# A hybrid attention and state-space block in f32: the state-space branch's output product by one level of Strassen's scheme

## The chip, the cores and the metric

One Trainium2 chip; the kernel runs on one of its cores. The metric is the device time of one execution in microseconds (us), the median over several runs. The engines are TensorE (PE in the profile), VectorE (DVE), ScalarE (ACT), GpSimd (POOL) and SyncE (SP, which here only issues DMAs).

## The reference

One layer of a token mixer with three branches (latent attention "mla", forgetting attention "fox", a state-space scan "ssm"), each with its own output matrix and sigmoid gate, followed by a gated feed-forward part. Sequence length and model width are 1024; the two attention branches are 512 wide, the state-space branch 1024. What matters here:

```python
y_a = mla_branch(...) @ w_br_mla[l]        # [1024, 512]  @ [512, 1024]
y_b = fox_branch(...) @ w_br_fox[l]        # [1024, 512]  @ [512, 1024]
y_c = ssm_branch(...) @ w_br_ssm[l]        # [1024, 1024] @ [1024, 1024]
g = jax.nn.sigmoid(u_gate + b_gate[l]).reshape(Bsz, S, N_BRANCH, D_MODEL)
merged = g[:, :, 0] * y_a + g[:, :, 1] * y_b + g[:, :, 2] * y_c
x = x + merged @ w_out[l]
```

`ssm_branch` ends in an RMS norm with a gain per column (`norm_g`); everything is float32.

## The kernel before, in words

**Precision.** A float32 operand is used as two rounded tiles, a high part and a low part (`split`, L139: ACT copies the high part, DVE subtracts it for the low part). A product of two such operands is three matmul passes, high x high, high x low and low x high (`mm3`, L161, one matmul on L167). Each matmul here is 128 x 128 weights on 128 x 512 data.

**Before the stage.** The attention results wait in DRAM (`att_d`), and so do the gates (`g_d`) and the rows of the state-space branch (`ys_d`, stored transposed by L1219 in eight blocks of 128 tokens, the last of them just before the stage). Projections that were left over (`fill`, matmuls on L840, evacuated on L847) fill PE up to the first matmul of the stage.

**The stage that is changed** (L1244 to L1290) makes the merged rows, transposed: eight tiles `merged[j]` (`mg`) of 128 columns by 1024 tokens. It runs over the branches in the order fox, mla, ssm. For each branch the input rows are loaded (`ar`, L1257) and split into `ah` and `al` (L1260; for ssm with the norm's gain `pc_n` as a scale, L1261 and L1262). Then for each of the eight column tiles j the weights are loaded and split (`load_w`, L734: `wr`, `wh`, `wl`), the gate row is loaded (`gl`, L1272), and two halves of 512 tokens are computed: 12 matmuls each for fox and mla (4 blocks of 128 inputs x 3 passes), 24 for ssm. That is 192 + 192 + 384 = 768 matmuls, `ybr` in the profile. DVE evacuates each half, `(gate + 1) * psum` (L1279); for mla POOL adds it to `merged` (L1282), for ssm DVE does (L1284). In the ssm branch each finished row is at once rounded into `mh` and `ml` (the tiles `hnh` and `hnl`, L1285 and L1286), the operand of the output projection `wo`, which follows (weights `raw` loaded at L1394, split into `woh` and `wol`, matmuls on L1417).

**What sets the order.** In this stage a scheduler orders each engine's instructions; each engine then runs its own list strictly in order, and SP's list is the order in which DMAs are issued. A tile pool with n buffers makes the n+1-th tile wait for the readers of the first. `wr`, `wh` and `wl` have two buffers each, the pool with the tag `t4` (rows, gates) has four.

**Elsewhere in the kernel.** The feed-forward up projection already uses the seven-product scheme: its helper `product` runs the 12 matmuls of one block product, and `sums` (L1464 to L1470) lets POOL form the four sums of weight blocks.

## Time and profile before

| | |
|---|---|
| median of 3 runs | 2073.37 us (2071.99 to 2074.21) |
| profiled execution | 2070.99 us, its span 2069.3 us |
| granted TensorE clock, mean | 0.994 |
| busy share of the span | PE 97%, DVE 69%, ACT 46%, POOL 30% |
| moved by DMA | 303.62 MB, 147 GB/s on average |
| branch outputs of fox, mla and ssm | about 1151 to 1326 us, 8% of the chain |
| output projection and second norm | from 1326 us |

The span is what the profiler saw from the first to the last instruction; the execution's own time is 1.7 us longer. "The chain that ended last" follows the last instruction back to what released it, step by step. Each group row names the line, engine, operation and tiles, then how many instructions, busy time and mean duration, and at the end the idle time ahead of them and what ended it.

### The profile page before, as it was taken

Reading aid. Unit: us, or ns where it says so; the run is one execution under the profiler, and the core shown is the slowest. Engines: PE = TensorE matmul, PEld = TensorE weight load, DVE = VectorE, ACT = ScalarE, POOL = GpSimd, SP = SyncE. Lnnn points to the kernel's source line nnn. Section 1 sums busy time; section 2 is a strip of 40 time slices with the busy share of each in tenths; the row PEclk is TensorE's granted clock in tenths of the full one; section 3 lists DMA queues with packets and bytes.
Section 4 is the critical chain, followed back from the end, with each engine's and each line's share of the span. In section 5 each row is a group of like instructions: output and inputs, shape, how many; then the busy total and the mean of one; then the engine's idle time right before and its main releaser. Section 6 shows DMA issues by size and latency. Waiting matters only on the chain.

```text
span 2069.3 us, 29096 instructions
## 1 busy us (share of the span) xinstructions
PE 2014.6 (97%) x10265; PEld 1684.3 (81%) x10265; DVE 1425.6 (69%) x2595; ACT 950.5 (46%) x1739; POOL 616.9 (30%) x606
## 2 busy tenths in 40 slices
PE   6999899999999999999999999999899999999999
PEld 6989788788888888887778888888778888878887
DVE  5678579366667766757896355557987777775665
ACT  4555323156556666555554222323454444454432
POOL 2435233222222222210000040002654454422755
PEclk9999999999999999999999999999999999999999
DMA  5057878654344455324442665431222322329665
GB/s 175 18 175 252 261 225 248 199 158 142 105 126 110 134 133 133 101 82 135 134 134 82 217 207 167 154 121 63 84 89 81 95 79 72 102 88 338 231 227 195
DMA packets 276650, 303.62 MB, mean 147 GB/s; under 512 B 19308, under 2 KB 209784, under 8 KB 276504
## 3 DMA queue, kind: packets, MB, share of 16 engines
q1 hardware_dynamic: 276504, 301.76, 47.0%
q8 instruction: 81, 1.33, 0.3%
q14 instruction: 65, 0.53, 0.1%
HBM read 209.03 MB, written 92.67 MB: 146 GB/s over the span
## 4 chain that ended last, share of the span: by engine, by line
PE 84%; DVE 7%; DMA 5%; ACT 2%; issue 2%; SPq 0%; POOL 0%; DVEq 0%; ACTq 0%; POOLq 0%
PE mm L840 17%; PE dn L1703 10%; PE ybr L167 8%; PE ua L1371 5%; PE fx L167 5%; PE ud L1371 5%; PE uc L1371 5%; PE wo L1417 4%; PE s L930 4%; PE tp L999 3%; PE ub L1371 2%; PE fxv L167 1%; PE cq L167 1%; PE o L970 1%; PE kv L167 1%
## 5 line engine op out<-in xcount | busy, mean ns | idle before, releaser
L840 PE MATMUL mm<-hnh,wh 128*128 128x512 f32 x576 | 250.4, 435 | 0.0
L840 PE MATMUL mm<-hnh,wl 128*128 128x512 f32 x576 | 226.5, 393 | 0.0
L840 PE MATMUL mm<-hnl,wh 128*128 128x512 f32 x576 | 225.2, 391 | 0.0
L952 POOL TENSOR_SCALAR pm<-pm,rs 128x128 f32<-128x128 f32 (+7 forms) x128 | 107.9, 845 | 348.6 <-DVE rs L951 317.8
L1703 PE MATMUL dn<-dr,dr 128*128 128x512 f32 x592 | 182.2, 389 | 0.0
L1005 DVE TENSOR_TENSOR ptl<-tp,pth 128x512 fp32r<-128x512 f32 (+1 forms) x160 | 101.3, 633 | 83.8 <-ACT pth L1004 82.8
L935 DVE TENSOR_REDUCE nmx<-s 128x1 f32<-128x128 f32 (+2 forms) x192 | 105.7, 551 | 57.2 <-PE s L933 45.7
L945 ACT ACTIVATE pm<-s,nmx 128x128 f32<-128x128 f32 (+2 forms) x192 | 109.6, 575 | 55.9 <-DVE nmx L942 38.5
L1703 PEld LDWEIGHTS dn<-dr,dr 128*128 128x128 f32 x592 | 111.3, 188 | 23.0
L840 PEld LDWEIGHTS mm<-hnh,wl 128*128 128x128 f32 x576 | 108.0, 188 | 24.8
L840 PEld LDWEIGHTS mm<-hnl,wh 128*128 128x128 f32 x576 | 109.0, 189 | 18.4 <-issue 4.1
L840 PEld LDWEIGHTS mm<-hnh,wh 128*128 128x128 f32 x576 | 108.9, 189 | 17.8 <-issue 4.1
L1004 ACT ACTIVATE pth<-tp 128x512 fp32r<-128x512 f32 (+1 forms) x160 | 88.1, 551 | 69.4 <-PE tp L999 68.7
L930 PE MATMUL s<-qk,qk 96*128 96x384 f32 (+5 forms) x480 | 117.8, 350 | 0.9 <-ACT pm L945 0.9
L1282 POOL TENSOR_TENSOR mg<-mg,gl 128x512 f32<-128x512 f32 x16 | 24.9, 1558 | 306.5 <-DVE gl L1279 306.4
L1703 PE MATMUL dn<-dr 128*128 128x512 f32 x296 | 115.5, 390 | 0.0
L143 DVE TENSOR_TENSOR dr<-dr,dr 128x1024 fp32r<-128x1024 f32 x52 | 74.2, 1427 | 52.1 <-ACT dr L142 46.5
L167 PE MATMUL fx<-w5h,hnh 128*128 128x512 f32 x256 | 102.4, 400 | 1.7 <-ACT w5h L142 1.7
L167 PE MATMUL fx<-w5l,hnh 128*128 128x512 f32 x256 | 100.8, 394 | 2.0 <-DVE w5l L143 2.0
L167 PE MATMUL fx<-w5h,hnl 128*128 128x512 f32 x256 | 100.6, 393 | 0.0
L167 PE MATMUL ybr<-al,wh 128*128 128x512 f32 x256 | 99.2, 389 | 0.5 <-DVE al L143 0.5
L167 PE MATMUL ybr<-ah,wl 128*128 128x512 f32 x256 | 98.3, 389 | 0.0
(492 smaller groups left out, 5817.3 us busy)
## 6 DMA issues: line engine op xcount, KB each, us to landing
dr<-act_d SPq DMA_DIRECT2D x99, 256.0 KB
wr<-in_ffn_w_up_dram SPq DMA_DIRECT2D x47, 512.0 KB
wr<-in_w_in_dram SPq DMA_DIRECT2D x36, 512.0 KB
g_d<-t SPq DMA_DIRECT2D x24, 512.0 KB
gl<-g_d SPq DMA_DIRECT2D x24, 512.0 KB
ws<-in_ffn_w_down_dram SPq DMA_DIRECT2D x22, 512.0 KB
wsum_d<-ws SPq DMA_DIRECT2D x22, 512.0 KB
act_d<-fa SPq DMA_DIRECT2D x22, 512.0 KB
```

Source lines behind the costliest of these rows:

```text
L143: return i, le.tensor_sub(l, src, f32(h))
L167: T.matmul(ps, a(k), b(k), start=(i == 0), stop=(i == n - 1))
L840: T.matmul(ps, a[:, k, :], b[half][:, k, :], start=(k == 0 and i == 0), stop=(k == NK - 1 and i == 2))
L930: T.matmul(ps[:, :w], q_[:, qs], k_[:, a:a + w], start=i_ == 0, stop=not last and i_ == len(o.passes) - 1)
L935: later(c + 0.1, lambda ps=ps, ci=ci, a=a, b=b: V.reduce_max(nmx[:, ci:ci + 1], ps[:, :b - a], axis=AX, negate=True))
L945: pss[ci][1][0] = later(c + 0.9 + 0.1 * ci, lambda ci=ci, a=a, b=b: A.activation(p_[:, a:b], pss[ci][0][:, :b - a], AF.Exp, bias=nb, accum ...
L952: G.tensor_scalar(p_[:, 0:n * P], p_[:, 0:n * P], rs[:, 3:4], 0.0, op0=ALU.mult, op1=ALU.add)
L1004: later(c + 0.05, lambda th=th, pt=pt, off=off: A.activation(th[:, :off], pt[:, :off], AF.Copy))
L1005: pl[0] = later(c + 0.6, lambda th=th, tl=tl, pt=pt, off=off: V.tensor_sub(tl[:, :off], pt[:, :off], f32(th[:, :off])))
L1371: T.matmul(ps, a, b, start=first and n == 0, stop=n == 11, skip_group_check=not first)
L1417: T.matmul(p, a, b, start=k == 0 and i == 0, stop=k == NK - 1 and i == 2)
L1703: T.matmul(ps[m], a[:, ts_], b[:, 512:], start=first_ and j == 0 and q == 0, stop=j == NFH - 1 and q == 2, skip_group_check=not first_)
```

## The change

For pairs of column tiles (j, j + 4) and the two token halves, the ssm branch's four 128 x 512 outputs are made from seven block products instead of eight (Winograd's form of Strassen's scheme). A block product has 512 inputs: 12 matmuls. Four pairs x 7 x 12 = 336 matmuls take the place of 384. The scheme needs four sums of input blocks (`tsum`, made once) and four sums of weight blocks per pair (`S12`, `S34`), and its products are combined on the way out.

- **Token sums.** `tok_sums(n)`, called eight times (before fox column tiles 1 to 7 and before mla column tile 0), loads 128-column pieces of four blocks from `ys_d` into the one tile `tr` (pool with one buffer, two DMAs of 256 KB), scales them by the norm's gain on ACT, forms two differences on POOL and two on DVE, and splits the four results. The parts go into `mh` and `ml`, which stand empty until the merged rows are rounded.
- **Plain blocks.** `tok_block`, called six times (four in mla, two behind it), loads and splits the three unsummed blocks. The eight loads of full ssm rows are gone.
- **Pairs.** Each pair loads both weight tiles and both gate rows; POOL makes `S12` (in the buffer of `tr`) and `S34` (in a `t4` buffer). PE's order within the pairs is written by hand. Combining takes ACT copies out of PSUM, DVE and POOL adds, and the same gate multiply and merge add as before.
- **Rounding.** The merged rows stay in f32 until the last pair (`tail`), since `mh` and `ml` hold the token sums; all 16 roundings now stand in that pair.
- Helpers `product`, `rows` and `weight_sums` move up, and the feed-forward part uses them from there.

The core of the diff:

```diff
+        def tok_sums(n):
+            k, q = n // 2, n % 2 * 256
+            r = trp.tile([P, 4, 256], F32, name=uid("tr"), tag="tr")
+            for i in range(2):
+                SY.dma_start(r[:, 2 * i:2 * i + 2, :],
+                             ys_d[k + 4 * i].rearrange("p (h c) -> p h c", h=2)[:, :, q:q + 256])
+                A.activation(r[:, 2 * i:2 * i + 2, :], r[:, 2 * i:2 * i + 2, :], AF.Copy,
+                             scale=pc_n[:, k + 4 * i:k + 4 * i + 1])
+            a1, a2, b1, b2 = (r[:, i, :] for i in range(4))
+            G.tensor_sub(a1, a2, a1)
+            G.tensor_sub(a2, b2, a2)
+            V.tensor_sub(b2, b2, a1)
+            V.tensor_sub(b1, b1, b2)
+            for i, t in ((2, b2), (1, a1), (3, a2), (4, b1)):
+                h, l = (x_[k][:, q:q + 256] for x_ in tsum[i])
+                split(h, l, t)
...
             for j in range(NK):
-                wh, wl = load_w(fpl, wv[:, :, j * P:j * P + P], nk)
+                if b == 1 and j or b == 0 and j == 0:
+                    tok_sums(j - 1 if b else 7)
+                if b == 0 and 1 <= j < 5:
+                    k = 2 * (j - 1)
+                    blocks += tok_block(k, 0, k // 4)
+                wh, wl = load_w(fpl, wv[:, :, j * P:j * P + P], 4)
...
-                    if b == 2:
-                        V.tensor_add(m, m, g[:, hs])
-                        i0 = A.activation(mh[half][:, j, :], m, AF.Copy, scale=0.5)
-                        i1 = V.scalar_tensor_tensor(out=ml[half][:, j, :], in0=m, scalar=0.5,
-                                                    in1=f32(mh[half][:, j, :]), op0=ALU.mult, op1=ALU.subtract)
...
+                hA = operand(ri)
+                S12 = trp.tile([P, NK, P], F32, name=uid("S12"), tag="tr")
+                S34 = fpl.tile([P, NK, P], F32, name=uid("S34"), tag="t4", bufs=4)
+                weight_sums(S12, S34, ri, rj)
+                a0 = halfbank()
+                product(a0, hA, 0, *Y11)
+                A.activation(e1, a0, AF.Copy)
+                hS12 = operand(S12)
+                b0 = halfbank()
+                product(b0, hS12, 4, *tsum[2])
+                V.tensor_add(X, b0, e1)
+                if tail:
+                    rounded(range(3), 0)
+                product(a0, hA, 4, *Y21, first=False)
+                add(a0, j, 0)
+                if tail:
+                    rounded((3,), 0)
+                hS34 = operand(S34)
+                h22 = last22[:, 0:4, :], last22[:, 4:8, :]
+                split(*h22, rj[:, 4:8, :])
+                c0_ = halfbank()
+                product(c0_, hS12, 0, *tsum[1])
+                A.activation(e5, c0_, AF.Copy)
+                if tail:
+                    rounded((4, 5, 6), 0)
+                d0 = halfbank()
+                product(d0, hS34, 0, *tsum[3])
+                A.activation(e7, d0, AF.Copy)
+                G.tensor_add(Y, e5, e7)
+                G.tensor_add(Y, X, Y)
+                if tail:
+                    rounded(range(3), 1)
+                product(c0_, hS34, 4, *Y22, first=False)
+                V.tensor_add(e1, c0_, X)
+                add(e1, j, 1)
+                add(Y, j + 4, 1)
+                if tail:
+                    rounded((3,), 1)
+                product(d0, h22, 0, *tsum[4], first=False)
+                V.tensor_add(e5, d0, X)
+                add(e5, j + 4, 0)
+                if tail:
+                    rounded((7,), 0)
+                    rounded(range(4, NK), 1)
```

Since the scheduler decides the rest, here is how the instructions stand. First ACT at the start of fox, in the kernel before (`t` is an evacuated bank of the fill, `ah` the high part of an attention row, `wh` that of weights):

```order
L847 ACTIVATE t_4321_13365<-mm_13366,pc_g 128x512
L142 ACTIVATE ah_13470<-ar_13468 128x1024
L142 ACTIVATE ah_13476<-ar_13474 128x1024
L142 ACTIVATE wh_13530<-wr_13528 128x512
L847 ACTIVATE t_4321_13365<-mm_13406,pc_g 128x512
L142 ACTIVATE ah_13482<-ar_13480 128x1024
```

The same place in the changed kernel; `op` is now the name of a row's high part, and L1284 is the scaling in `tok_sums`:

```order
L847 ACTIVATE t_4321_13365<-mm_13366,pc_g 128x512
L142 ACTIVATE wh_13559<-wr_13557 128x512
L847 ACTIVATE t_4321_13365<-mm_13406,pc_g 128x512
L1284 ACTIVATE tr_13540<-tr_13540,pc_n 128x512
L142 ACTIVATE op_13482<-ar_13480 128x1024
L142 ACTIVATE op_13488<-ar_13486 128x1024
L142 ACTIVATE op_13494<-ar_13492 128x1024
L1284 ACTIVATE tr_13540<-tr_13540,pc_n 128x512
L142 ACTIVATE hnh_13476<-tr_13540 128x256
L142 ACTIVATE hnh_13477<-tr_13540 128x256
L142 ACTIVATE op_13500<-ar_13498 128x1024
```

The fill's last evacuation and the first scaling of `tr` moved ahead of the first row's split, on which PE's first branch matmul waits. On SP the two loads of `tr` stand behind the last store to `ys_d` and three of the four row loads:

```order
L1219 DMA ys_d<-yT_13259 128x8x128
L1312 DMA ar_13480<-att_d_82 128x1024
L1312 DMA ar_13486<-att_d_82 128x1024
L1312 DMA ar_13492<-att_d_82 128x1024
L1282 DMA tr_13540<-ys_d 128x2x256 x2
L854 DMA g_d_80<-t_4321_13365 128x1024
L734 DMA wr_13663<-in_w_br_fox_dram 128x4x128
L1312 DMA ar_13498<-att_d_82 128x1024
```

Before, all four row loads followed the store directly; `tr` reads what that store writes. Last, ACT in the last pair of the ssm branch in the changed kernel (L1383 copies product 1 out, L1351 rounds a merged row, `woh` are the output weights, `S_4538` is `S34`):

```order
L1383 ACTIVATE op_14304<-ybr_14724 128x512
L1351 ACTIVATE hnh_13476<-mg_13454 128x512
L1351 ACTIVATE hnh_13476<-mg_13455 128x512
L1351 ACTIVATE hnh_13476<-mg_13456 128x512
L142 ACTIVATE woh_14909<-raw_14911 128x512 x2
L142 ACTIVATE woh_14909<-raw_14917 128x512 x2
L142 ACTIVATE wh_14778<-S_4538_14719 128x1024
L1351 ACTIVATE hnh_13476<-mg_13458 128x512
```

Three roundings and four splits of output weights stand ahead of the split of `S34`, whose product is the fifth of the pair. On DVE the low parts of the same tiles stand in the same order.

More of the change, by code (lines that the diff above doesn't have):

```diff
@@ L1282, in block_kernel @@
                         G.tensor_add(m, m, g[:, hs])
[L1283 to L1289 removed]
+        for k in (4, 6):
+            blocks += tok_block(k, 1, 2)
@@ L1364, in halves @@
         return h, l
-    def product(ps, hl, k0, rh, rl, first=True):
-        n = 0
-        for k in range(4):
-            h, l = hl[0][:, k0 + k, :], hl[1][:, k0 + k, :]
-            for a, b in ((h, rh[k]), (h, rl[k]), (l, rh[k])):
-                T.matmul(ps, a, b, start=first and n == 0, stop=n == 11, skip_group_check=not first)
-                n += 1
     def bank(name):
@@ L1442, in block_kernel @@
                 norm2(t - 1, x2r[t - 1])
-    def rows(t, k0):
-        return [t[:, k0 + k, :] for k in range(4)]
     B11, B21 = [(rows(h2h[0], k), rows(h2l[0], k)) for k in (0, 4)]
```

90 lines of the change are left out of this document (71 added, 19 removed).

## The prediction

> **What bounds the kernel now.** I read the page's head first, then the busy time by windows over the stage that the change touches, then the chain that ended last through it.
>
> ```profile
> span 2069.3 us, 29096 instructions
> PE 2014.6 (97%) x10265; PEld 1684.3 (81%) x10265; DVE 1425.6 (69%) x2595; ACT 950.5 (46%) x1739; POOL 616.9 (30%) x606
> ```
>
> TensorE is busy for 97% of the span. That is an average; the windows show the stage itself (columns after the window: its length, then busy time and count of PE, weight load, DVE, ACT, POOL; then PE clock, DMA share, GB/s).
>
> ```profile
> 1151.00:1240.00 89.00, 88.54 (x391) 73.04 (x390) 45.87 (x59) 22.08 (x28) 21.46 (x15) 1.00 0.66 209
> 1240.00:1326.00 86.00, 86.00 (x381) 71.19 (x381) 48.74 (x63) 26.21 (x35) 3.40 (x2) 1.00 0.47 150
> ```
>
> PE is idle for 0.46 us of 175. DVE is busy about 55% of it, ACT 28%, POOL 14%, and the clock is full. The chain says the same, and shows how the stage begins:
>
> ```profile
> 1144.16 5.65 DMA ar<-att_d
> 1149.83 1.07 ACT ah L142
> 1150.92 1.24 DVE al L143
> 1152.20 173.92 PE ybr L167 x766
> 1326.12 27.20 PE wo L1417 x120
> ```
>
> So matmuls alone set the stage's length: 173.92 us / 766 = 0.227 us each. Every matmul left out is worth 0.227 us, as long as nothing new makes PE wait. The change must be read for such waits, and its margin is small.
>
> **What is removed.** The state-space branch falls from 384 matmuls (8 column tiles x 2 halves x 24) to 336 (4 pairs x 7 products x 12): 48 x 0.227 = **-10.9 us**, all of it on the path.
>
> **The fox start.** Before, the stage starts as soon as the first attention rows are split. The new first token-sum step has its scaling on ACT ahead of the fox rows' splits, and it reads what the last `ys_d` store writes.
>
> ```profile
> 1143.75 0.36 SPq L1219 DMA_DIRECT2D ys_d<-yT  x1
> 1144.16 8.34 SPq L1257 DMA_DIRECT2D ar<-att_d  x4
> ```
>
> ACT and PE at the same place:
>
> ```profile
> 1152.66 0.67 ACT L847 ACTIVATE t<-mm,pc_g 128x512 f32<-128x512 f32 x1
> 1153.23 1.05 ACT L142 ACTIVATE ah<-ar 128x1024 fp32r<-128x1024 f32 x1
> ```
>
> ```profile
> 1151.12 0.62 PE L167 MATMUL ybr<-ah,wh 128*128 128x512 f32 x2
> 1152.20 0.50 PE L167 MATMUL ybr<-al,wh 128*128 128x512 f32 x1 [0.46 <-DVE al L143]
> ```
>
> How long such a store takes to land is seen at an earlier one, which ACT waits for:
>
> ```profile
> 1125.13 0.36 SPq L1219 DMA_DIRECT2D ys_d<-yT  x1
> ```
>
> ```profile
> 1128.42 1.06 ACT L1203 ACTIVATE yT<-y 128x1024 f32<-128x1024 f32 x1 [3.31 <-DMA ys_d<-yT]
> ```
>
> That is 3.3 us on quiet queues. The store of 1143.75 therefore lands at 1147.1 or later, the read is issued then, behind three 512 KB row loads of which the first took 5.65 us, and I put its first half at 1152 to 1154. On ACT the evacuation of the last fill bank now also stands ahead (it waits for the fill's last matmul, just ahead of PE's first row below, and takes 0.67, so it ends near 1152.2). Then come the scaling (0.6, as other 128x512 copies on ACT below) and the first row split (1.05). PE's first branch matmul moves from 1151.12 to about 1154.8; 0.3 to 0.5 us of wait for the low part follow in both kernels. I take **+3.3 us**, between +2 (read at 1152.2, no queueing) and +5 (read near 1155).
>
> **Token sums through fox and mla.** Eight steps run beside 16 units of 48 matmuls (10.9 us each). Each is two loads of 256 KB, two scalings, two POOL and two DVE subtractions and four splits, and the next one's loads wait until the single `tr` buffer is free. Beside them the later `ar` reads are replaced by half-row blocks; in all 3 MB more are read.
>
> ```profile
> L142 ACT ACTIVATE wh<-wr 128x512 fp32r<-128x512 f32 x15 | 9.4, 629 | 47.1 <-PE ybr L167 47.1
> L143 DVE TENSOR_TENSOR wl<-wr,wh 128x512 fp32r<-128x512 f32 x15 | 11.0, 736 | 0.0
> L1282 POOL TENSOR_TENSOR mg<-mg,gl 128x512 f32<-128x512 f32 x16 | 24.9, 1558 | 306.5 <-DVE gl L1279 306.4
> ```
>
> Transfers of 512 KB, issue against first reader:
>
> ```profile
> 1296.09 0.37 SPq L1394 DMA_DIRECT2D raw<-in_w_out_dram  x1
> 1302.69 0.37 SPq L1394 DMA_DIRECT2D raw<-in_w_out_dram  x1
> ```
>
> ```profile
> 1300.70 1.16 ACT L142 ACTIVATE woh<-raw 128x512 fp32r<-128x512 f32 x2 [5.11 <-DMA raw<-in_w_out_dram]
> 1306.51 1.15 ACT L142 ACTIVATE woh<-raw 128x512 fp32r<-128x512 f32 x2 [1.23 <-DMA raw<-in_w_out_dram]
> ```
>
> So 4.6 and 3.8 us. One step as a chain: load 4.6, scalings 2 x 0.63, POOL 2 x 1.56, DVE 2 x 0.74, four high splits at 0.63 and a last low one at 0.74: 13.7 us if the 128x256 pieces cost as much as 128x512 ones, 9.4 us if everything but load and scalings costs half. The half sizes are the nearer row, so I take about 10.5, just under one unit. Steps that start after the late first one (ends near 1162) then finish near 1232, before the first product that reads a sum (about 1245). Weights of a unit stand behind a step in SP's queue but are loaded about a unit ahead; I find 2.6 to 4 us to spare at each. POOL and ACT are idle for three quarters of this window. **0** (0 to +10; below nothing is excluded since PE has no idle time there to win back).
>
> **The product ends of the state-space pairs.** A product takes 12 x 0.227 = 2.72 us, but its weights are split only when one of two buffers is free. The third weight set of a pair (`hS34`) gets its buffer when the third product ends, and is needed one product (2.72 us) later. This is what follows a product's end now, its last matmul first, then DVE:
>
> ```profile
> 1271.33 0.39 PE L167 MATMUL ybr<-ah,wl 128*128 128x512 f32 x1
> ```
>
> ```profile
> 1271.76 0.69 DVE L1279 SCALAR_TENSOR_TENSOR gl<-gl,ybr 128x512 f32<-128x512 f32 x1 [2.58 <-PE ybr L167]
> 1272.48 0.69 DVE L1284 TENSOR_TENSOR mg<-mg,gl 128x512 f32<-128x512 f32 x1
> 1273.09 1.22 DVE L143 TENSOR_TENSOR wl<-wr,wh 128x1024 fp32r<-128x1024 f32 x1
> ```
>
> In pairs 0 to 2 the same three stand there: 0.43 after the last issue (1271.33) begins the first, then 0.72, 0.61 and 1.22 are 2.98 us, and the low part is needed 2.72 + 3 x 0.227 = 3.40 after it. About 0.4 us is left: **0**, 0 to +0.4 each. In pair 0 the second product's low part is late by some **+0.3**, since ACT and DVE come from the last mla units and row blocks.
>
> The weight sums are made by POOL; their cost is seen in the up stage, which forms the same sums:
>
> ```profile
> L1470 POOL TENSOR_TENSOR S<-wr,S 128x512 f32<-128x512 f32 x16 | 28.4, 1773 | 0.0
> L1469 POOL TENSOR_TENSOR S<-wr,wr 128x512 f32<-128x512 f32 x8 | 18.1, 2268 | 8.1 <-DVE wl L143 8.1
> ```
>
> **The last pair.** Here roundings of finished rows and the splits of the output weights stand ahead of `hS34`'s split on ACT and DVE. These weights reuse the `wr` buffers, which POOL's last sums release. Counted from the pair's first matmul: POOL's S34 can start once the previous pair's first gate buffer has been merged, at about +1.7; its halves end at 1.7 + 2.3 = 4.0 and 4.0 + 1.8 = 5.8; the two loads land 3.8 to 4.6 us later, at 8.2 and 9.6 to 10.4. ACT does two 128x512 splits per load (1.15): the second pair ends at 11.5, `hS34`'s high part at 12.6, its low part 1.2 later at 13.8. PE wants the high part at 4 x 2.72 = 10.9 (1.7 late) and the low part three matmuls on (another 0.8): **+2.5 us**, ends +0.9 (second load at 9.6, one copy faster) and +4.
>
> **The end of the stage.** About thirty DVE operations of 0.6 to 0.7 us follow late in the last pair. By the same counting the last rounded row is ready some 0.9 us before the output product wants it: **0** (0 to +2). The later stages are unchanged.
>
> **Sum:** -10.9 + 3.3 + 0 + 0.3 + 2.5 + 0 = **-4.8 us**. The profiled execution took 2070.99 us (span 2069.3), 2.4 us less than the runs' median of 2073.37; so 2066.2 on its own basis and **2068.6** on the median's. A measurement of this kernel can tell about 0.2%, 4.1 us, from no change: the forecast stands just beyond it, below 2069.2.
>
> **The rivals.**
>
> *All new waits hidden.* If the first read lands by 1151 and the last pair's loads early, only -10.9 is left: **2062.5**. For it: PE's gap-free stage with ACT at 28%. Against it: the read must follow a store that takes 3.3 us.
>
> *Slower: the token-sum chain paces the stage.* One `tr` buffer and an in-order SP queue: if a step takes the 13.7 us of the upper bound instead of 10.9, seven follow-ups fall 7 x 2.8 = 20 us behind; about 4 us are to spare, and the rest, +16, is handed to PE by weights that queue behind the waiting load. Net -4.8 + 16 = +11: **2084.6**. It decides from 11.5 us a step. For it: POOL took 1.56 us for 128x512 beside DVE, and the DMA share is already 0.66. Against it: the pieces are half that size.
>
> *DVE slowed beside POOL.* The 0.4 us of slack at the fifth product is gone where POOL's sums make DVE slower:
>
> ```profile
> L143 DVE TENSOR_TENSOR wl<-S,wh 128x1024 fp32r<-128x1024 f32 x32 | 51.1, 1597 | 17.9 <-ACT wh L142 17.9
> L143 DVE TENSOR_TENSOR wl<-wr,wh 128x1024 fp32r<-128x1024 f32 x15 | 18.3, 1218 | 0.0
> ```
>
> The same operation takes 1.60 us in the up stage where its source is a sum that POOL forms, 1.22 on a loaded tile. With 0.38 us more on the split and as much on the merge add, each of the four pairs loses about 0.4 us at the fifth product, and as much at the second: +3, **2071.6**. [...]
>
> *The clock drops at the gap.* PE would stand idle for some 3.6 us at the fox start. The trace has both outcomes (windows, then the wait in the last of them):
>
> ```profile
> 30.00:40.00 10.00, 5.12 (x28) 4.16 (x27) 6.22 (x41) 4.42 (x20) 0.00 (x0) 0.91 0.55 162
> 40.00:50.00 10.00, 10.00 (x52) 9.91 (x52) 6.54 (x19) 3.93 (x7) 4.77 (x2) 0.75 0.16 52
> ...
> 1480.00:1500.00 20.00, 16.23 (x72) 13.13 (x71) 19.96 (x15) 7.61 (x9) 15.29 (x8) 1.00 0.26 84
> ```
>
> ```profile
> PE uc L1371 <- ACT e L1585: 5.6, 2, 3.8
> ```
>
> After a half-idle stretch the clock is 0.75 over 10 us, which costs 2.5 us; after a single wait of up to 3.8 us in the up stage it stays 1.00. With a drop: -4.8 + 2.5, **2071.1**. [...]
>
> **How the numbers follow.** Chances: forecast 0.45, all hidden 0.22, DVE slowed 0.14, clock 0.07, chain paces 0.12. The forecast's own range, 2066 to 2072 with its terms' ends partly cancelling, lies on both sides of 2069.2: 0.28 faster, 0.17 same. The all-hidden case is faster (0.22). DVE and clock are nearly all "same" (0.12 and 0.06), with 0.03 slower. The pacing case is slower in 0.10 and the same in 0.02. Faster 0.50, same 0.37, slower 0.13. The range goes from 2061.5 (all hidden, with 1 us of scatter) to 2078 (pacing at half its price); some 0.15 is left out.
>
> **What would show it.** In the changed profile: about 718 branch matmuls recorded, of 0.227 us between the fox start and `wo`; a first branch matmul at 1154 to 1156 with ACT's scaling of `tr` behind a DMA; no PE wait on weights in fox and mla; in the last pair one PE wait of 1 to 4 us on ACT's or DVE's split of the second sum, behind the output weights' loads; POOL's sums at 1.3 to 2.3 us. I am wrong if PE waits on weight loads at unit after unit, if no gap stands at the fox start, or if the stage has gaps at each pair.

## The result and the profile after

The changed kernel takes **2090.34 us** (median; 2084.80 to 2094.78), the kernel before 2073.37 us in the same comparison (five runs, 2068.75 to 2074.21). The ratio is **1.0082, interval [1.0066, 1.0098]**: some 17 us slower, where 4.8 us faster had been forecast. The profiled execution took 2088.56 us.

The page's head and busy times:

```profile
span 2085.8 us, 29257 instructions
PE 2014.0 (97%) x10202; PEld 1681.0 (81%) x10217; DVE 1475.1 (71%) x2667; ACT 983.3 (47%) x1811; POOL 664.8 (32%) x646
```

TensorE has 48 matmuls less to do and yet is busy as long as before (2014.0 against 2014.6 us): for part of the time its clock was lower (down to 0.50, rows below). And the span is 16.5 us longer: it also waits. All its waits in the stage, from its timeline (start, duration, line, tiles, count; in brackets the idle time ahead and what ended it):

```profile
1155.20 2.50 PE L167 MATMUL ybr<-op,wh 128*128 128x512 f32 x5 [3.36 <-ACT op L142]
1170.56 0.50 PE L167 MATMUL ybr<-op,wl 128*128 128x512 f32 x1 [0.73 <-DVE wl L143]
1206.18 0.96 PE L167 MATMUL ybr<-op,wh 128*128 128x512 f32 x3 [0.19 <-ACT op L142]
1217.10 1.19 PE L167 MATMUL ybr<-op,wh 128*128 128x512 f32 x4 [3.14 <-ACT wh L142]
1220.52 0.80 PE L167 MATMUL ybr<-op,wl 128*128 128x512 f32 x1 [2.23 <-DVE wl L143]
1245.56 0.50 PE L167 MATMUL ybr<-op,wl 128*128 128x512 f32 x1 [0.84 <-DVE wl L143]
1260.12 0.50 PE L1249 MATMUL ybr<-hnh,wh 128*128 128x512 f32 x1 [1.12 <-ACT wh L142]
1263.47 0.79 PE L1249 MATMUL ybr<-hnh,wl 128*128 128x512 f32 x1 [2.61 <-DVE wl L143]
1331.23 0.50 PE L1249 MATMUL ybr<-hnh,wh 128*128 128x512 f32 x1 [1.23 <-ACT wh L142]
1332.84 0.51 PE L1249 MATMUL ybr<-hnh,wl 128*128 128x512 f32 x1 [0.87 <-DVE wl L143]
1352.35 0.50 PE L1540 MATMUL wo<-woh,hnl 128*128 128x512 f32 x1 [0.86 <-DVE hnl L1352]
```

They make 17.2 us, against 0.46 before: 3.4 at the start of fox, 7.1 within fox and mla, 3.7 at the first pair's second product, 2.1 in the last pair, 0.9 at the output product. L1249 is now the matmul of a block product, L167 that of fox and mla. The clock in the windows that hold a drop (length; busy time and count of PE, weight load, DVE, ACT, POOL; PE clock, DMA share, GB/s):

```profile
1150.00:1155.00 5.00, 1.84 (x9) 1.18 (x7) 0.69 (x1) 2.72 (x4) 0.72 (x1) 0.88 0.93 347
1155.00:1160.00 5.00, 4.80 (x11) 3.80 (x12) 4.82 (x6) 3.66 (x7) 1.48 (x2) 0.50 0.81 280
1160.00:1165.00 5.00, 5.00 (x22) 4.08 (x21) 2.46 (x5) 1.28 (x3) 0.00 (x0) 0.93 0.84 321
1215.00:1220.00 5.00, 1.19 (x4) 0.67 (x4) 3.44 (x3) 3.50 (x7) 3.56 (x3) 0.87 0.27 105
1220.00:1225.00 5.00, 4.48 (x11) 3.51 (x12) 5.00 (x9) 1.12 (x3) 1.39 (x1) 0.50 0.63 199
1225.00:1230.00 5.00, 5.00 (x22) 4.11 (x21) 4.58 (x6) 2.40 (x4) 2.58 (x3) 0.95 0.86 258
1260.00:1265.00 5.00, 2.27 (x6) 1.54 (x7) 5.00 (x3) 1.07 (x3) 5.00 (x4) 0.81 0.60 207
1265.00:1270.00 5.00, 5.00 (x20) 4.05 (x19) 0.79 (x2) 0.00 (x0) 2.47 (x2) 0.85 0.71 212
```

At each of the three places with the longest waits TensorE goes on with a reduced clock: 11 matmuls in 4.8 us where 22 fit into 5.0. Busy time times the missing share of the clock, added over the eight rows, is 6.8 us.

For what follows, "the stage" runs from the end of the fill's last matmul (its start and the pitch of 0.227 us) to the second norm's first transpose. It takes 202.0 us before and 217.4 after; what follows it takes 716.1 and 716.8. The books: -10.9 for the matmuls, +16.7 for the waits (17.2 less the 0.46 of before), +6.8 for the clock are +12.6; measured is +15.4. Each of the eleven restarts costs a little more (a single matmul takes 0.39 us, one in a row 0.227: 11 x 0.16 = 1.8); 1.0 stays unassigned.

**Where the 7 us within fox and mla come from.** SP's loads for the token sums, the first and the last of the eight steps, two DMAs each:

```profile
1148.14 1.26 SPq L1282 DMA_DIRECT2D tr<-ys_d  x2
...
1237.23 1.18 SPq L1282 DMA_DIRECT2D tr<-ys_d  x2
```

The seven intervals mean (1237.23 - 1148.14) / 7 = 12.7 us; the longest, ahead of the seventh step, is 17. What ACT waits for in this time, in the view of waits:

```profile
ACT tr L1284 <- DMA tr<-ys_d: 20.3, 9, 5.9
```

The scaling of `tr` stops ACT's in-order list nine times, for 20.3 us. At the largest wait of TensorE, ACT, then DVE and POOL:

```profile
1213.24 0.72 ACT L1284 ACTIVATE tr<-tr,pc_n 128x512 f32<-128x512 f32 x1 [1.87 <-DMA tr<-ys_d]
1215.50 0.72 ACT L1284 ACTIVATE tr<-tr,pc_n 128x512 f32<-128x512 f32 x1 [1.54 <-DMA tr<-ys_d]
1216.13 0.40 ACT L142 ACTIVATE hnh<-tr 128x256 fp32r<-128x256 f32 x1
1216.43 0.61 ACT L142 ACTIVATE wh<-wr 128x512 fp32r<-128x512 f32 x1
```

```profile
1216.56 0.81 DVE L143 TENSOR_TENSOR hnl<-tr,hnh 128x256 fp32r<-128x256 f32 x1 [3.16 <-ACT hnh L142]
1217.29 1.51 DVE L1289 TENSOR_TENSOR tr<-tr 128x256 f32<-128x256 f32 x1
1218.72 1.74 DVE L143 TENSOR_TENSOR wl<-wr,wh 128x512 fp32r<-128x512 f32 x1
```

```profile
1217.05 2.87 POOL L1336 TENSOR_TENSOR mg<-mg,gl 128x512 f32<-128x512 f32 x2
```

The weights' high part (`wh`, 1216.43) stands behind two scalings that wait for loads; TensorE goes on right behind it, at 1217.10. The low part (`wl`) follows two operations of the sums on DVE, slowed while POOL's merge add runs: 1.74 us instead of the 0.736 that its group has before, and 1.51 for a 128x256 difference. TensorE waits for it to 1220.52.

### The profile page after: what moved, and what is told of

It is laid out like the page before. It is cut to its first block, busy times and chain, and to the rows that moved or that the text cites. A ratio compares the mean times of both kernels' runs of the same rounds, so it can differ in the third digit from the quotient of the medians.

```text
span 2085.8 us, 29257 instructions
## 1 busy us (share of the span) xinstructions
PE 2014.0 (97%) x10202; PEld 1681.0 (81%) x10217; DVE 1475.1 (71%) x2667; ACT 983.3 (47%) x1811; POOL 664.8 (32%) x646
## 4 chain that ended last, share of the span: by engine, by line
PE 73%; DVE 10%; DMA 9%; issue 3%; POOL 3%; ACT 2%; SPq 0%; DVEq 0%; POOLq 0%; ACTq 0%
PE mm L840 16%; PE dn L1820 10%; PE ua L1249 5%; PE uc L1249 5%; PE ud L1249 5%; PE fx L167 5%; PE s L930 4%; PE wo L1540 4%; PE ub L1249 2%; PE tp L999 2%; DMA att_d<-o 2%; DMA tr<-ys_d 1%; PE fxv L167 1%; PE cq L167 1%; PE q L167 1%
## 5 line engine op out<-in xcount | busy, mean ns | idle before, releaser
L167 PE MATMUL fx<-w5h,hnh 128*128 128x512 f32 x256 | 102.7, 401 | 1.7 <-ACT w5h L142 1.7
L167 PE MATMUL fx<-w5l,hnh 128*128 128x512 f32 x256 | 101.1, 395 | 2.5 <-DVE w5l L143 2.5
L1256 POOL TENSOR_TENSOR S<-wr 128x512 f32<-128x512 f32 x25 | 36.7, 1469 | 203.9 <-DVE wl L143 151.2
L167 PE MATMUL fx<-w5h,hnl 128*128 128x512 f32 x256 | 100.8, 394 | 0.0
L1287 POOL TENSOR_TENSOR tr<-tr 128x256 f32<-128x256 f32 x8 | 6.2, 779 | 292.4 <-ACT tr L1284 292.4
L142 ACT ACTIVATE wh<-S 128x1024 fp32r<-128x1024 f32 x50 | 53.0, 1060 | 86.7 <-PE uc L1249 55.1
```

The costliest lines, as they stand in the source:

```text
L167: T.matmul(ps, a(k), b(k), start=(i == 0), stop=(i == n - 1))
```

## The experiments

**Theory.** The token sums pace fox and mla: their loads come one step at a time through one buffer and one in-order queue, and the weights' splits stand behind them. **Rivals.** The sums' work on ACT, DVE and POOL costs the time, whatever the loads do; or the start of fox does, its gap and the clock after it. All kernels were compared with the kernel before on the same chip, where its median was 2070.4 to 2073.4 us, so medians of different rows are not to be subtracted. The stage is that of the one profiled execution; it is read for differences of several us, the ratios for the verdicts. Up to the end of the fill these executions differ by 8 us (1149 to 1158), so a stage and a ratio need not agree.

| kernel | median us | ratio to before, interval | stage us |
|---|---|---|---|
| before | 2073.37 | 1 | 202.0 |
| after | 2090.34 | 1.0082 [1.0066, 1.0098] | 217.4 |
| e_resident | 2076.07 | 1.0025 [1.0016, 1.0034] | 203.5 |
| e_nosums | 2078.53 | 1.0037 [1.0023, 1.0051] | 203.4 |
| e_loads | 2081.59 | 1.0055 [1.0033, 1.0076] | 212.2 |
| e_warm | 2084.73 | 1.0071 [1.0054, 1.0089] | 213.6 |
| e_pool0 | 2087.28 | 1.0076 [1.0060, 1.0092] | 217.4 |
| e_poolw | 2090.78 | 1.0089 [1.0076, 1.0102] | 221.8 |
| e_blocks | 2090.79 | 1.0094 [1.0080, 1.0107] | 220.7 |
| e_combo | 2096.08 | 1.0116 [1.0101, 1.0132] | 227.8 |
| e_mgfirst | 2093.30 | 1.0096 [1.0079, 1.0114] | 219.0 |
| e_mla_dve | 2086.30 | 1.0072 [1.0058, 1.0085] | 215.4 |
| e_order | 2096.95 | 1.0119 [1.0104, 1.0135] | 228.9 |
| e_order_dve | 2099.48 | 1.0132 [1.0116, 1.0147] | 231.1 |
| e_slots | 2087.43 | 1.0074 [1.0061, 1.0087] | 218.7 |
| e_pace | 2086.09 | 1.0073 [1.0061, 1.0085] | 217.7 |
| e_pace2 | 2081.36 | 1.0046 [1.0033, 1.0059] | 212.0 |
| e_pace_dve | 2079.55 | 1.0037 [1.0024, 1.0051] | 207.5 |
| e_pace_warm | 2081.21 | 1.0045 [1.0031, 1.0058] | 211.3 |

### Loads or work

**e_resident** keeps every operation of the sums and takes only their loads away: the scaling reads an attention row that is on the chip.

```diff
-                SY.dma_start(r[:, 2 * i:2 * i + 2, :], ys_d[...][:, :, q:q + 256])
-                A.activation(r[:, 2 * i:2 * i + 2, :], r[:, 2 * i:2 * i + 2, :], AF.Copy, scale=...)
+                src = f32(ah[i])[:, 0:512].rearrange("p (h c) -> p h c", h=2)
+                A.activation(r[:, 2 * i:2 * i + 2, :], src, AF.Copy, scale=...)
```

> The token sums are formed from two attention rows that lie in SBUF instead of from loads of ys_d, so they are not the reference's; all their work on ACT, POOL and DVE stays, only the 16 loads into tr are gone. Theory 1 (ACT and DVE stand in order behind steps that wait for tr's loads): the waits of PE in fox and mla go (3.4 + 0.7 + 0.2 + 3.1 + 2.2 + 0.8 = 10.4 us in the changed kernel's trace) and with them two drops of the clock (about 5 us): some 2075 us. Theory 2 (the work itself, POOL's operations slowing DVE's beside them): only the gap at the fox start goes, about 6 us with its clock drop: some 2084 us, and PE still waits at the mla start by 4 to 5 us.

**e_nosums** leaves the sums out altogether (`tsum = {1: Y21, 2: Y11, 3: Y22, 4: Y11}`, no `tr` in fox and mla).

> No token sums at all: the four products that read them read plain blocks (so the result is not the reference's), neither loads nor sums are made; pairs, their products and the late rounding stay. Theories 1 and 2 both: fox and mla run as in the kernel before, and with 48 matmuls fewer only pair 0 and the last pair cost: 2066 to 2070 us. Rival (the pairs themselves are the loss: weight sums, buffers, rounding): above 2080 us, with the waits in the pairs.

**e_loads** is e_nosums with the sixteen loads into `tr` kept, read by nobody.

> As the run without token sums (four products read plain blocks, so the result is not the reference's), but the 16 loads into tr are issued where they stand in the changed kernel, and nothing reads them. Stage length is taken from the fill's last matmul to the first transpose of the second norm: 202.0 us before, 217.4 changed, 203.4 without token sums. Theory 1 (ACT and DVE stand in order behind tr's loads): 203 to 205, as without them. Rival 1b (the loads themselves crowd the queues, so that weights and gates land late): 208 or more, with PE's waits ended by weights whose loads are late.

TensorE's waits in the stage, first of e_resident, then of e_nosums (total, times, longest):

```profile
PE ybr L1249 <- DVE wl L143: 3.2, 2, 2.3
PE ybr L167 <- ACT op L142: 2.2, 1, 2.2
PE ybr L167 <- DVE wl L143: 1.7, 1, 1.7
PE ybr L1249 <- ACT wh L142: 1.4, 1, 1.4
PE wo L1538 <- DVE hnl L1350: 0.8, 1, 0.8
```

```profile
PE ybr L1249 <- DVE wl L143: 2.3, 1, 2.3
PE ybr L167 <- ACT op L142: 2.2, 1, 2.2
PE wo L1539 <- DVE wol L143: 2.2, 1, 2.2
PE wo L1539 <- ACT woh L142: 0.5, 1, 0.5
```

Without the loads, the sums' work leaves a single wait of 1.7 us in fox and mla and a stage as long as without any sums (203.5 and 203.4 us). Its median, 2076.07, is where theory 1 had it (2075), and its interval lies below that of the changed kernel. So it isn't the work alone: without the loads the waits go. What the loads do by themselves is less clear. In e_loads the stage is 8.8 us longer than in e_nosums (212.2 against 203.4; 3.1 of them are clock, which by the same count of windows costs 6.2 against 3.1 us), but the intervals of the two ratios overlap (its runs go from 2075.05 to 2094.82), and since nothing reads `tr`, its loads come sooner than in the changed kernel: all are issued by 1191 us, there by 1238. Busy time and DMA share from 1155 to 1195, of e_nosums and of e_loads:

```profile
1155.00:1195.00 40.00, 37.73 (x159) 30.42 (x158) 17.32 (x23) 9.96 (x13) 0.00 (x0) 0.96 0.60 199
```

```profile
1155.00:1195.00 40.00, 39.70 (x167) 32.42 (x168) 15.30 (x21) 7.68 (x11) 0.00 (x0) 0.96 0.84 275
```

The DMA share goes from 0.60 to 0.84 (0.65 in the changed kernel), and after 1195 TensorE waits on weights five times, 3.7 us together. Whether crowded transfers or places in SP's queue delay the weights, and how much of either there is in the changed kernel, these runs don't part.

The second lesson is in e_nosums: even without sums the kernel isn't faster than before; 2066 to 2070 us had been expected. Start of fox (2.2), first pair (2.3), output product (2.7) and clock (3.1) are 10.3 us, as much as the 48 matmuls gave.

### The start of fox and the clock

**e_pool0** lets POOL do the first step's scaling, so that none stands ahead of the rows' splits on ACT.

```diff
+                if n == 0:
+                    G.tensor_scalar_mul(half_, half_, g)
+                else:
+                    A.activation(half_, half_, AF.Copy, scale=g)
```

> The first token-sum step is scaled on POOL instead of ACT, so ACT's first split of an attention row no longer stands behind the load of tr; the other seven steps stay. If the gap at the fox start is that wait: first branch matmul back at about 1 us behind the fill's end, no cold clock there, 5 to 6 us less than the changed kernel: 2084.5. Rival (the late first step only hands its wait on to the next weights, since tr's single buffer is free later): a wait of 2 us or more on weights within the first three units, and 2088 to 2090.

The wait fell from 3.36 to 2.21 us, where about 1 had been expected, the stage not at all: waits came back later (2.27 and 1.78 in mla's third and fourth unit, a unit being one column tile). The remaining 2.21 us are there in e_resident, e_nosums and e_loads too, where no scaling waits for a load. In the program the first row's split also waits for the fill's last evacuation (`t`, L847). **e_mgfirst** opens the pools of the merged rows ahead of those of the operands (two lines change places); **e_slots** opens the operand pools in another order:

```diff
-        slots = [pe_.enter_context(TP(f"slot{i}", 1)) for i in range(4)]
+        slots = {i: pe_.enter_context(TP(f"slot{i}", 1)) for i in (1, 0, 2, 3)}
```

> The pools of the merged rows are opened ahead of the operand slots, nothing else; the program then no longer makes the first fox row's split wait for the fill's last evacuation, and ACT's list has it ahead of the first scaling of tr again. If the fox start is lost to that memory order (the 2.2 us wait that stays without any load of tr) and to the scaling (1.1 us more), with a clock drop of some 3 us behind the gap: stage 211 to 212 us instead of 217.4, no cold clock at 1155 to 1165. Rival (the later waits take it up, since the first step now ends later): 215 us or more.

> Only the order in which the four operand slots are opened is changed (1, 0, 2, 3). The first fox row's split no longer waits for the fill's last evacuation, and in the last pair the second weight sum's split now stands ahead of the output weights' splits, which still come early. Pace theory (a step of 9 to 12 us against units of 5.4 us; what is saved at the start comes back as waits in mla): stage 212 to 219 us, no gap at the fox start, waits of 8 us or more in mla. If the losses are independent: 217.4 - 6 at the start - 2 in the last pair = 209 us.

With e_mgfirst the gap at the start is gone and with it the slow clock there (matmuls every 0.22 to 0.23 us from the first one at 1157.56 on). But fox's last unit and mla wait ten times, 10.1 us together, and the output product 6.3 us for its weights; e_order and e_order_dve below, with the same order of pools, have that wait too (by the program, the merged rows then hold these weights' memory until they are rounded). In e_slots 2.1 us are left at the start, on other releasers, and fox's last unit and mla get 8.5, as the pace theory had it. The time won at the start comes back as waits in mla.

**e_warm** puts 32 matmuls of the identity (64 instructions of together 7.3 us in the trace; 3.5 us had been counted on) between the fill and the first branch matmul.

```diff
+            warm = psp.tile([P, 512], F32, name=uid("warm"), tag="half")
+            for _ in range(32):
+                T.matmul(warm[:, 0:P], ident, ident, start=True, stop=True)
```

> 32 idle 128x128 matmuls of the identity are put between the fill's last matmul and the first branch matmul, about 3.5 us of PE work in the 3.4 us gap; nothing else is changed. If the granted clock of 0.5 at 1155 to 1160 us follows from PE's idleness and costs time of its own: 2 to 3 us less than the changed kernel (some 2087.5), the clock 1.00 there. If the drop costs nothing because the rows' splits set the pace there: the same time, 2090, or up to 0.5 us more.

TensorE starts the branch 7.1 us after the fill instead of 3.5, and the stage is still 3.8 us shorter: the clock stays up at the start (matmuls every 0.22 to 0.23 us from 1156.38 on), and the sums have gained a start of 3.6 us (the mla waits fall to 4.7 us). But the ratio's interval overlaps that of the changed kernel, and the profiled execution (2081.91) is the shortest of its six: a gain isn't shown.

### Moving the work away

**e_poolw** splits the weights of fox and mla on POOL, and moves POOL's two differences of each step to DVE.

```diff
-            G.tensor_sub(a1, a2, a1)
-            G.tensor_sub(a2, b2, a2)
+            V.tensor_sub(a1, a2, a1)
+            V.tensor_sub(a2, b2, a2)
...
-                wh, wl = load_w(fpl, wv[:, :, j * P:j * P + P], 4)
+                wh, wl = load_w(fpl, wv[:, :, j * P:j * P + P], 4, G, G)
```

> In fox and mla the weights are split on POOL, both parts, and the token sums' two POOL subtractions move to DVE; loads and sums stay whole. No weight stands behind a token sum on ACT or DVE any more. Theory 1: PE's waits in the middle of fox and mla (0.7 + 0.2 + 3.1 + 2.2 + 0.8 us) and the cold clock at 1220 go, the fox start (3.4) and the pairs (5.8) stay: stage some 207 to 209 us. Rival 2 (DVE is slowed beside POOL, which is now busier): waits on weights of 5 us or more remain, 214 to 220.

The theory's expectation failed (221.8 us, where 207 to 209 had been expected): TensorE now waits for POOL's low parts (3.38 and 2.39 us) and the attention rows of mla. **e_blocks** moves the last two plain blocks behind the first pair's third product.

```diff
-        for k in (4, 6):
-            blocks += tok_block(k, 1, 2)
...
+                if j == 0:
+                    for k in (4, 6):
+                        blocks += tok_block(k, 1, 2)
```

> The two row blocks that only the sixth product reads are loaded and split in the first pair, behind its third product, instead of between mla and the pairs. If they are what stands ahead of the first weight sum's split (waits of 1.1 + 2.6 us at the first pair's second product, and a colder clock behind them): these fall to 1 us or less, stage some 213 to 214 us. If POOL's late weight sum is the cause (its two halves stand behind merge adds): unchanged within 1 us.

The first pair's waits at product 2 fall from 3.7 to 1.8 us, and 6.8 us appear at product 5 (3.74 and 3.05), so the stage is longer, not shorter. **e_combo** joins both and lets DVE make the high parts of the first three attention rows of fox (`split(h, l, raw, V if b and k < 3 else A)`).

> Weights of fox and mla split on POOL, the two late blocks moved behind the first pair's third product, and the first three fox rows' high parts made on DVE instead of ACT. By theory 1 with the clock: no gap at the fox start, none in fox and mla, pair 0 within 1 us, the last pair's 2.1 us stay: stage 194 to 197 us, so 5 to 8 us below the kernel before: 2063 to 2066. If DVE is too loaded by that: 200 to 205 us, the same as before.

Its stage is 227.8 us, far above both expectations, and its median above either's. **e_mla_dve** does mla's merge adds on DVE, so that none of POOL's runs beside DVE's splits (`V.tensor_add(m, m, g[:, hs])`).

> mla's merge adds move from POOL to DVE (0.69 us each there). If POOL's work beside it is what slows DVE at the mla start and ahead of the first pair (weights' low parts at 1.7 and 2.3 us instead of 0.7 and 1.2): the waits on DVE there, 2.2 + 0.8 + 2.6 us, fall to 2 us together, stage some 212 us. If these waits come from late loads and the order alone: within 1.5 us of 217.4, or more for the longer DVE list.

It brings 2 us of the stage, and an interval that overlaps that of the changed kernel. The waits on DVE named there fall from 5.7 to 3.7 us: those in mla to 0.7, while the first pair's stays (3.04).

### Pacing

**e_order** writes ACT's and DVE's order through fox and mla by hand, one step beside each of units 1 to 8 and each load issued a unit ahead, pools as in e_mgfirst (`units` are the eight column tiles of fox, then those of mla). **e_order_dve** adds the merge adds on DVE.

```diff
+        ctx_m = tc.manual_schedule(engines={mybir.EngineType.Activation, mybir.EngineType.DVE})
+        ctx_m.__enter__()
+        for u, (b, j) in enumerate(units):
+            if u + 1 < 16 and u + 1 not in W:
+                W[u + 1] = weights(u + 1)
+            if 1 <= u <= 8:
+                tok_sums(u - 1, nr)
...
+            if u <= 7:
+                nr = tok_load(u)
```

> The pools as in e_mgfirst, and through fox and mla ACT's and DVE's orders are written by hand: next weights first, then the token sum whose load was issued a unit ahead, then row splits, then the evacuation; loads, sums and products are those of the changed kernel. Theory 1 (the order: work that waits for a late load stands ahead of weights): no gap at the fox start and none in fox and mla, no clock drop there; the pairs' waits (3.7 and 2.1 us) stay or fall: stage 194 to 199 us, about 2063 to 2070 us. Rival 1b (the loads crowd the queues in any order): 203 us or more, waits on weights in mla remain.

> As e_order, with mla's merge adds on DVE instead of POOL. If POOL slows DVE ahead of the first pair: 1 to 3 us less than e_order, the first pair's wait on DVE gone. Else the same within 1 us, or slower by the longer DVE list.

With e_combo they are the slowest; where theory 1 had 194 to 199 us for e_order, its stage takes 228.9. SP's and ACT's waits in e_order:

```profile
SPq L1282 <- DVE hnl L143: 36.0, 7, 6.9
```

```profile
ACT tr L1289 <- DMA tr<-ys_d: 23.1, 14, 3.1
```

The load is ready to go and waits 36 us for the buffer, then ACT 23 us for the load. From the second on, steps follow each other every 8.2 to 9.3 us, while a unit of fox, 24 matmuls, takes 24 x 0.227 = 5.4 us. With one buffer, one step per unit doesn't fit even in this order: TensorE waits at unit after unit. **e_pace** gives each step two units (slots as in e_slots, merges on POOL); **e_pace2** spreads the steps so that the last isn't late:

```diff
+        STEPS = (1, 3, 5, 6, 8, 10, 11, 13)
...
-            if 1 <= u <= 8:
-                tok_sums(u - 1, nr)
+            if u in STEPS:
+                tok_sums(STEPS.index(u), nr)
...
-            if u <= 7:
-                nr = tok_load(u)
+            if u + 1 in STEPS:
+                nr = tok_load(STEPS.index(u + 1))
```

> ACT and DVE ordered by hand in fox and mla as in e_order, with the slots as in e_slots, but one token-sum step every two units (10.9 us) instead of every unit (5.4 us); loads, sums and products as in the changed kernel. Pace theory: a step (8.5 to 9.3 us in e_order) now fits, PE waits less than 2 us in fox and mla; the last step ends with mla, so the first pair may wait 2 to 5 us: stage 195 to 200 us, some 2064 to 2069 us. Rival (the volume of loads crowds the queues whatever the pace): 205 us or more, with waits on weights spread over mla.

> As e_pace, with the eight steps in units 1, 3, 5, 6, 8, 10, 11 and 13 (1.7 units, 9.3 us each), so that the last ends two units ahead of the first pair. Pace theory: little slack, waits of 0 to 3 us in fox and mla, and the first pair's wait below e_pace's: stage 194 to 201 us. Rival: as for e_pace, 205 us or more.

In e_pace the waits within fox and mla are 3.1 us (7.1 after; 2.7 at the start not counted), but the last step ends so late that the first pair waits 9.07 us. In e_pace2 they are 3.3, with 4.3 in the first pair. Its interval lies below that of the changed kernel; that of e_pace overlaps it. So slower steps halve the waits in the middle, but both stages (217.7 and 212.0) miss what the pace theory had (195 to 200, 194 to 201) and lie in the range of its rival (205 or more), that the volume of loads crowds the queues. What waits remain in the middle are on weights, in mla: the rival isn't excluded. **e_pace_dve** moves mla's merge adds to DVE on top, **e_pace_warm** adds eight matmuls of the identity at the start.

> The schedule with eight evenly spread token-sum steps (stage 212.0 us from the fill's last matmul to the second norm's first transpose, where before has 202.0), and the mla merges' four additions per row group moved from POOL to DVE. Theory 1 (the first pair's waits of 3.34 and 0.95 us come from POOL, whose merges stand ahead of the sum of the first pair's second product and slow DVE beside them): these waits fall to about 1 us and DVE's 128x512 sums of that place to their usual time, the stage is 207 to 210 us, the kernel about 2078 us, ratio 1.002 to 1.004. Theory 2 (they come from the load of the weight block, or DVE has no room for the merges): the first pair's waits stay over 3 us or the mla half's grow, the stage is 211 us or longer, the ratio 1.0045 or more.

> The same, with eight matmuls of the identity by itself between the fill's last product and the first product of the output, their results read by nobody. Theory 1 (the clock of 0.50 for 6.5 us at the start follows from the two waits of about 2.5 us together): TensorE is idle less there, the granted clock stays at 0.8 or more from the start to the fourth unit, and the stage is 2 to 3 us shorter than without the eight. Theory 2 (the clock is set by something else, or the matmuls only push the rest back): the clock drops all the same or the stage is as long.

In e_pace_dve the ratio is where theory 1 had it, but not for its reason: the first pair still waits 4.5 us: 1.48 at its first product for the high part of weights whose load came late (ACT had waited 3.94 us for it), and 2.98 at its second for the low part of the sum, behind DVE's merge adds and plain blocks, no longer behind POOL's merge adds; fox and mla wait 1.5 us instead of 3.3, and the clock did not drop at the start (1.00 in the rows below). The profiled execution of e_pace_dve (2074.40) is the shortest of its runs, that of e_pace_warm (2084.18) the longest, so their stages exaggerate; by their ratios the two don't differ, and the eight matmuls show nothing. No version tried beats the kernel before; e_pace_dve comes nearest of those that leave nothing out.

How the clock goes on after like waits is best seen in the start of e_pace2 and of e_pace_dve, in rows of one microsecond:

```profile
1157.00:1158.00 1.00, 0.72 (x4) 0.26 (x2) 0.00 (x0) 0.55 (x1) 0.00 (x0) 1.00 1.00 382
1158.00:1159.00 1.00, 0.00 (x0) 0.00 (x0) 0.00 (x0) 1.00 (x3) 0.00 (x0) 1.00 0.89 314
1159.00:1160.00 1.00, 0.73 (x2) 0.30 (x2) 0.94 (x2) 1.00 (x3) 0.00 (x0) 1.00 0.11 38
1160.00:1161.00 1.00, 0.05 (x1) 0.06 (x1) 1.00 (x2) 0.56 (x1) 0.00 (x0) 0.58 0.58 229
...
1166.00:1167.00 1.00, 1.00 (x4) 0.80 (x3) 0.74 (x1) 0.22 (x1) 0.00 (x0) 0.51 0.84 328
1167.00:1168.00 1.00, 1.00 (x6) 0.78 (x5) 0.48 (x1) 0.00 (x0) 0.00 (x0) 1.00 1.01 414
```

```profile
1151.00:1152.00 1.00, 0.00 (x0) 0.00 (x0) 0.00 (x0) 1.00 (x2) 0.00 (x0) 1.00 0.68 242
1152.00:1153.00 1.00, 0.59 (x2) 0.30 (x2) 0.61 (x1) 1.00 (x3) 0.00 (x0) 1.00 0.15 51
1153.00:1154.00 1.00, 0.14 (x1) 0.00 (x0) 1.00 (x2) 0.88 (x1) 0.00 (x0) 1.00 0.24 94
1154.00:1155.00 1.00, 0.73 (x3) 0.64 (x4) 1.00 (x2) 0.00 (x0) 0.00 (x0) 1.00 1.08 365
```

In e_pace2 two waits, 1.36 and 1.13 us with two matmuls between, bring the clock to 0.50: a row of 0.58 is 0.84 us at half, so from 1160.16, and 0.51 in the row from 1166 puts the end at 1166.98. In e_pace_dve two waits at the same place, 1.77 and 1.13 us, bring no drop (1.00 throughout). What parts the two was not shown.

## Why the prediction was wrong, step by step

- **What is removed, -10.9: held.** 2014.6 - 10.9 + 6.8 of lost clock + 1.8 of restarts = 2012.3 us of PE time; the page has 2014.0, 1.7 us unaccounted for. (Outside the stage the clock fell at other places than before, too.)
- **The fox start, +3.3: held in size** (3.36, first branch matmul at 1155.20, "1154 to 1156" was expected), but only partly in cause. ACT had both causes in its list, the scaling and the evacuation ahead of the first split. The prediction leaned on the read of `ys_d`; e_pool0 and e_nosums show that 2.2 us stay without it, and e_mgfirst that another order of the pools removes them.
- **Token sums through fox and mla, 0: this step failed.** "Eight steps run beside 16 units of 48 matmuls (10.9 us each)" is wrong: fox and mla have 192 + 192 matmuls, so a unit has 24 and takes 5.4 us. "About 10.5, just under one unit" was in truth just under two. The sixteen units last 87 us, which eight steps of 10.5 nearly fill; at the 12.7 us measured they overrun it. The 2.6 to 4 us to spare at each unit are less than the 5.5 us by which a unit is shorter. The waits were 7.1 us, and e_resident shows whose they are: without the loads, 1.7 remain. Two smaller slips stand in the same paragraph: the lower bound of a step is 9.8 with the load of 4.6 us that the upper one has (9.4 needs their mean, 4.2), and seven steps of 10.5 us behind 1162 end at 1235, not 1232.
- **The product ends, 0: held** in the pairs between, where TensorE never waits. **Pair 0's second product, +0.3: 3.7 in its place.** The prediction named the cause, "ACT and DVE come from the last mla units and row blocks", and mis-sized it. The late units of the token sums explain only part: at the same place e_nosums and e_resident still wait 2.3 us. DVE there, then POOL:

```profile
1257.99 3.22 DVE L1302 SCALAR_TENSOR_TENSOR op<-ar,pc_n,op 128x512 fp32r<-128x512 f32 x2 [0.94 <-ACT op L1301]
1261.13 2.28 DVE L143 TENSOR_TENSOR wl<-S,wh 128x1024 fp32r<-128x1024 f32 x1
```

```profile
1256.03 1.58 POOL L1256 TENSOR_TENSOR S<-wr 128x512 f32<-128x512 f32 x1 [3.06 <-DMA wr<-in_w_br_ssm_dram]
...
1258.94 5.60 POOL L1336 TENSOR_TENSOR mg<-mg,gl 128x512 f32<-128x512 f32 x3
```

  POOL waits 3.06 us for the weight block, then forms the sum, and DVE does the plain blocks and the low part beside POOL's merge adds, 2.28 us for what takes 1.22 on a loaded tile. With mla's merges on DVE 3.3 us remain (e_mla_dve), with the slower steps as well 4.5 (e_pace_dve), 3.0 of them behind DVE's own queue. That POOL's merge adds alone cost this wait is refuted; a single cause was not found.
- **The last pair, +2.5: held** (1.23 + 0.87 = 2.1, on the high and low part of `S34`, as described; the prediction's own times give 0.5 and not 0.8 for the low part, so 2.2). **The end of the stage, 0: 0.9**, inside its bound of 2.
- **The rivals.** *The chain paces the stage* had a chance of 0.12 and comes nearest: e_resident shows that the waits in the middle hang on the sums' loads, though pace and crowding were not parted. It was to "decide from 11.5 us a step", and with the right unit it decides from about half of that. Its price for the pacing, 16 us, is near the sum of the 10.8 us of waits in fox, mla and the first pair and most of the clock's 6.8, which it left out. *The clock drops at the gap* came true as well, at three places instead of one and at 6.8 us instead of 2.5. The kernel before's one wait of 3.8 us at a clock of 1.00 was no sign of what the gap would bring here: waits of 3.36 and 3.14 us, and one of 2.61, came with a drop (last section). *DVE slowed beside POOL* is seen in the rows (1.74 for 0.74, 2.28 for 1.22), mostly where mla's merges run, and e_mla_dve puts its price at about 2 us of the stage, not shown by the ratios.

The first failure has a plain root: a number of the stage, matmuls per unit, was not divided through once more. With 5.4 us in its place the prediction's own 10.5 us per step says that steps called beside successive units fall behind by 5 us at each. The clock's 6.8 us follow the waits. The first pair's wait has more causes than this one, as 2.3 us of it are there without any sums.

## What to carry to other kernels

Before removed matmuls are booked as a gain, work out the cover that one loop turn of TensorE gives (matmuls in it by their pitch) and set against it the whole round trip that a single buffer allows: load, use, release, next load. Taking the loads away (e_resident, which leaves out the true operands) removed the waits here; moving work between engines mostly moved them. And a saving of a few microseconds is easily eaten by three gaps of 2 to 3 us: here the lowered clock at the three places cost another 6.8 us.

## What the runs showed of the hardware

- The clock fell to 0.50 and stayed there for 6.8 us though TensorE was busy again: 1160.16 to 1166.98 in e_pace2, and 1153.84 to 1160.66 in the changed kernel, worked out in the same way from rows of one microsecond (0.92 from 1153 to 1154, 0.67 from 1160 to 1161). The changed kernel's other two drops run from 1218.69 to 1225.52 and from 1263.06 to 1266.48 (0.84 and 0.74, 0.53 and 0.76 in the rows at their ends): 6.8 and 3.4 us.
- When it fell at the start, TensorE had been idle for 2.0 us in the changed kernel (since 1151.84) and for 1.7 of the last 2.4 in e_pace2, where no wait was longer than 1.4 us; 2.9 us in two waits passed without a drop in e_pace_dve, and so did the kernel before's single wait of 3.8 us (3.77 ahead of 1487.26; the clock is 1.00 from 1480 to 1500). The length of the wait alone doesn't part the two outcomes; what does was not shown.
- Beside POOL's merge adds DVE took 2.28 us for a split of 128x1024 instead of 1.22, and 1.51 us for a 128x256 difference instead of 0.41, the median: 1.9 and 3.7 times as long. Of the eight differences of L1289 the three beside POOL took 1.51 us, the five others 0.41 to 0.42, and no split, difference or plain block of the changed kernel's stage took longer than usual while POOL was idle. Not everything beside POOL was slower: the gate multiply of L1333 took 0.67 to 0.69 us there as well, and the split of 128x1024 at 1311.87 took 1.22 beside POOL's weight sum.
